# Two of four weight sums added in the transfer, and one block's gating issued after the down round beside it

## The chip, the cores and the metric

The kernel runs on one core of a Trainium2 chip. The metric is the time of one execution on the device in microseconds (us), lower is better. The work is in float32 throughout, and every product is made of three matrix multiplications on split operands, so the result stays near float32 accuracy.

## The reference, cut to what matters

Two layers over 512 tokens of width 1024. Each has a token mixer (layer 0 a spatial gating unit, layer 1 a gated linear recurrence), and then the channel mixer that the change is about:

```python
def conv_ffn(h, w_up, conv_w, conv_b, w_down):      # h: 512 x 1024, w_up: 1024 x 6144, w_down: 3072 x 1024
    up = causal_dwconv(h @ w_up, conv_w, conv_b)    # width 3, per channel
    gate, val = jnp.split(up, 2, axis=-1)
    return (jax.nn.gelu(gate) * val) @ w_down

for i in range(2):
    x = x + mixer(rms_norm(x, norm_mix[i]))
    x = x + conv_ffn(rms_norm(x, norm_ffn[i]), ...)
return rms_norm(x, norm_final)
```

## The kernel before, in words

Features lie on the 128 partitions, the 512 tokens along the free axis. Every float32 operand is split into a high part (a cast to fp32r, `nc.scalar.copy`, on ACT) and a low part (what the cast left out, `tensor_tensor` subtract, on DVE), and a product is high*high + high*low + low*high on PE.

**Up blocks.** `conv_ffn` makes the 3072 hidden channels in 12 blocks, q = 0 to 11. `up(q)` runs 96 matmuls of 512 columns into 4 PSUM banks (gate and value, two groups of 128 channels each). DVE multiplies each bank by the norm factor `rbc` into a tile `up`; ACT and DVE make the width-3 convolution into a tile `cv` (one ACT operation, two DVE `scalar_tensor_tensor`); ACT applies gelu to the gate, and DVE multiplies gate and value into `yr`. `input_sums` then adds and subtracts quarters of `yr` and splits seven of them into the tile `y` (one ACT cast, one long DVE subtract).

**Down rounds.** `down(qs, ...)` multiplies six blocks by `f_w_down` in Winograd's form of Strassen's scheme: `seven` makes 7 products instead of 8, each into its own PSUM bank, of sums of the four quarters of the weights and sums of the four quarters of the input. There are three such rounds: layer 0 after block 6 (blocks 0 to 5) and after block 11 (blocks 6 to 11), and layer 1 after block 6 (blocks 0 to 5). Blocks 6 to 11 of layer 1 go through an ordinary product, `project_out`. Each round runs twice (m = 0, 1) over half of the output columns; a round has 12 chunks, one for each m and block. The names say which: `d0010` is layer 0, the round that begins with block 0, m = 1, block 0, and `d06010` is layer 0, the round that begins with block 6, m = 0, block 10. A chunk is 42 matmuls of 256 columns: 18 read its part a (plain quarters), then 24 its part b (sums of quarters).

**Weights of a chunk.** `weight_sums` loads the four quarters into a tile `raw` (here `d0010r`) by two transfers on the queue of SP, makes four sums on DVE (`d0010s`: one operation over 512 columns, two over 256), and splits part a (three quarters, 768 columns) and part b (four sums, 1024 columns) into `d0010ahi`, `d0010alo`, `d0010bhi`, `d0010blo`. `raw`, high and low tiles each come from a ring of three buffers, which the weights of the up blocks (`fu060r` and so on) use as well. Parts a and b take turns in the ring, so part b of a chunk gets its buffer when PE has read part a of the chunk before it, and part a of a chunk when PE has read part b of the chunk two before it.

**After a round.** Banks are added into the residual `xall` in 11 operations of DVE with two scratch tiles `e` and `u` and two ACT copies.

**Order.** The program is written in one order; a scheduler sets each engine's queue at build time by priorities, and `tc.high_priority` moves weight splitting and the first reads of the banks ahead. On the chip each engine runs its queue strictly in order, and an instruction that waits holds up all behind it.

## Time and profile before

| | |
|---|---|
| median of 3 runs | 1345.16 us (1344.72 to 1346.21) |
| profiled execution, its own time | 1344.57 us |
| its span, first to last instruction | 1342.8 us |
| PE busy | 1319.3 us, 98% of the span |
| DVE busy | 955.9 us, 71% |
| ACT busy | 595.2 us, 44% |
| POOL busy | 12.0 us, 1% |
| mean granted clock of PE | 0.997 of full speed |
| moved by transfers | 129.30 MB, mean 96 GB/s |

PE is busy almost all the time, and the rest of the span is short waits. A time on the chip is the span and some 1.8 us around it. A busy share says little about a stretch: DVE is at 71% over the span, and far above that in some stretches of some 35 us, which the rows below show.

### The profile page before, as it was taken

What the parts mean: (1) busy time and instruction counts of PE and PEld (TensorE: products, weight loads), DVE (VectorE), ACT (ScalarE), POOL (GpSimd) and SP (SyncE); (2) the same over time, 40 slices, a digit from 0 to 9 for tenths busy, and PEclk for the clock granted to TensorE, in tenths of its full rate; (3) what the DMA queues carried; (4) which work ended last, traced back from release to release, by engine and by line L of the source; (5) the groups of instructions that cost most, each with busy time, mean ns of one, the idle gap of its engine ahead of it and who ended that gap; (6) DMA issues with size and microseconds to landing.
All of it is one profiled execution on the core that took longest, in us unless ns stands there. A gap on an engine that the chain in (4) does not pass through costs nothing.

```text
span 1342.8 us, 16731 instructions
## 1 busy us (share of the span) xinstructions
PE 1319.3 (98%) x6510; PEld 1103.8 (82%) x6510; DVE 955.9 (71%) x1336; ACT 595.2 (44%) x773; POOL 12.0 (1%) x20
## 2 busy tenths in 40 slices
PE   9999999999999989999899999999999999999997
PEld 7888888888888988888887888888888899888886
DVE  7227775447878886878987799954687888676735
ACT  6455332334444433444453678633344443343432
POOL 1010000000000000000000000000000000000000
PEclk9999999999999999999999999999999999999999
DMA  6333222222222223222232333223222222422221
GB/s 231 93 94 108 80 79 94 95 94 94 94 95 87 84 82 126 94 92 71 90 118 87 94 94 94 94 97 102 85 94 94 94 79 95 126 94 94 92 82 63
DMA packets 106127, 129.30 MB, mean 96 GB/s; under 512 B 6464, under 2 KB 80192, under 8 KB 106048
## 3 DMA queue, kind: packets, MB, share of 16 engines
q1 hardware_dynamic: 105904, 128.23, 29.8%
q8 instruction: 51, 0.84, 0.3%
q14 instruction: 28, 0.23, 0.1%
q10 hardware_dynamic: 144, 0.00, 0.0%
HBM read 126.11 MB, written 2.10 MB: 95 GB/s over the span
## 4 chain that ended last, share of the span: by engine, by line
PE 90%; DVE 7%; issue 2%; ACT 1%; DVEq 0%; POOLq 0%; POOL 0%; ACTq 0%
PE f L111 13%; PE f L112 13%; PE f L113 13%; PE u L111 2%; PE v L374 2%; PE v L375 2%; PE u L113 2%; PE u L112 2%; PE v L376 2%; PE aop L111 2%; PE aop L113 2%; PE aop L112 2%; PE d001m L515 2%; PE d101m L515 2%; PE bx L113 2%
## 5 line engine op out<-in xcount | busy, mean ns | idle before, releaser
L458 DVE SCALAR_TENSOR_TENSOR cv<-up,vt,cv 128x511 f32<-128x511 f32 (+1 forms) x192 | 141.4, 746 | 20.8 <-ACT cv L456 19.7
L456 ACT ACTIVATE cv<-up,vt 128x512 f32<-128x512 f32 x96 | 77.7, 811 | 84.2 <-DVE up L542 84.2
L542 DVE TENSOR_TENSOR up<-f,rbc 128x512 f32<-128x512 f32 x96 | 65.2, 684 | 0.0
L495 DVE TENSOR_TENSOR y<-yr,y 128x1792 fp32r<-128x1792 f32 x18 | 36.5, 2025 | 13.8 <-ACT y L494 13.8
L546 ACT ACTIVATE cv<-cv 128x512 f32<-128x512 f32 x48 | 30.2, 629 | 33.6 <-DVE cv L458 33.0
L494 ACT CAST y<-yr 128x1792 fp32r<-128x1792 f32 x18 | 30.4, 1690 | 14.1 <-DVE yr L492 8.5
L434 DVE SCALAR_TENSOR_TENSOR sv<-sv,vt,bs 128x256 f32<-128x256 f32 x32 | 15.0, 478 | 19.1 <-PE sv L431 19.1
L211 ACT ACTIVATE xh<-xall,vt 128x512 fp32r<-128x512 f32 x24 | 17.0, 717 | 21.9 <-DVE xall L263 15.9
L220 ACT ACTIVATE sq<-xall 128x512 f32<-128x512 f32 (+1 forms) x37 | 21.4, 586 | 9.8 <-DVE xall L275 9.8
L458 DVE SCALAR_TENSOR_TENSOR xb<-xr,vt,xb 128x511 f32<-128x511 f32 (+2 forms) x36 | 25.5, 744 | 0.1
L548 DVE TENSOR_TENSOR yr<-cv 128x512 f32<-128x512 f32 x36 | 24.8, 688 | 0.8
L221 DVE TENSOR_TENSOR acc<-acc,sq 128x512 f32<-128x512 f32 (+1 forms) x37 | 23.8, 643 | 2.0 <-ACT sq L220 1.9
L212 DVE SCALAR_TENSOR_TENSOR xl<-xall,vt,xh 128x512 fp32r<-128x512 f32 x24 | 17.9, 747 | 3.4 <-ACT xh L211 3.2
L552 ACT CAST y<-cv 128x512 fp32r<-128x512 f32 x12 | 7.4, 620 | 27.5 <-DVE cv L550 23.6
L226 POOL TENSOR_TENSOR rc<-ms,mhalf 128x4 f32<-128x4 f32 (+1 forms) x6 | 5.4, 904 | 1237.3 <-DVE ms L225 1237.3
L430 PE MATMUL sv<-ws,vh 128*128 128x256 f32 x64 | 15.4, 324 | 0.0
L436 DVE SCALAR_TENSOR_TENSOR sv<-sv,vt 128x256 f32<-128x256 f32 x32 | 15.0, 479 | 0.4
L431 PE MATMUL sv<-ws,vl 128*128 128x128 f32 x64 | 14.2, 222 | 0.0
L681 DVE TENSOR_TENSOR_SCAN hs<-riyh,sq 128x512 f32<-128x512 f32 x12 | 14.0, 1208 | 0.0
L490 DVE TENSOR_TENSOR yr<-yr 128x512 f32<-128x512 f32 x18 | 12.5, 692 | 0.6
L86 ACT ACT_TABLE_LOAD x10 | 12.8, 1283 | 0.1
L431 PEld LDWEIGHTS sv<-ws,vl 128*128 128x128 f32 x64 | 12.2, 191 | 0.5
(2559 smaller groups left out, 4475.1 us busy)
## 6 DMA issues: line engine op xcount, KB each, us to landing
xall<-xT SPq DMA_DIRECT2D x8, 256.0 KB, 5.2
outT<-o SPq DMA_DIRECT2D x8, 256.0 KB, 2.2
av00raw<-a_w_in SPq DMA_DIRECT2D x2, 256.0 KB, 3.9
av01raw<-a_w_in SPq DMA_DIRECT2D x2, 256.0 KB, 5.0
av02raw<-a_w_in SPq DMA_DIRECT2D x2, 256.0 KB, 5.6
av03raw<-a_w_in SPq DMA_DIRECT2D x2, 256.0 KB, 5.3
bs<-a_b_s SPq DMA_DIRECT2D x1, 512.0 KB, 6.0
av10r<-a_w_in SPq DMA_DIRECT2D x1, 512.0 KB, 6.6
```

The lines of the kernel that those rows point to most:

```text
L111: nc.tensor.matmul(ps, wh, xh, start=first, stop=False)
L112: nc.tensor.matmul(ps, wh, xl, start=False, stop=False)
L113: nc.tensor.matmul(ps, wl, xh, start=False, stop=last)
L374: nc.tensor.matmul(pss[c], xh[kk][:, ts], hi[:, k, :], start=kk == 0, stop=False)
L375: nc.tensor.matmul(pss[c], xh[kk][:, ts], lo[:, k, :], start=False, stop=False)
L456: nc.scalar.activation(dst, src, AF.Identity, scale=col(wname, woff + last * wstep), bias=col(cname, coff))
L458: nc.vector.scalar_tensor_tensor(dst[:, i:], src[:, :S - i], col(wname, woff + (last - i) * wstep), dst[:, i:], op0=ALU.mult, op1=ALU.add)
L494: nc.scalar.copy(hi, raw[:, 0:7])
L495: nc.vector.tensor_tensor(lo, raw[:, 0:7], hi.bitcast(F32), op=ALU.subtract)
L515: nc.tensor.matmul(banks[b][:, j], wt[:, w, js], xt, start=first and j == 0 and m == 0, stop=last and j == 1 and m == 2, skip_group_check= ...
L542: nc.vector.tensor_tensor(upt, pss[2 * half + j], rbc, op=ALU.mult)
L546: nc.scalar.activation(ts[0], ts[0], AF.Gelu_apprx_tanh)
```

## The change

`weight_sums` gets a tile of five slots in place of four. Write the quarters as (k, n). Two transfers on SP's queue each read one quarter and write it into two slots: (1,0) into slots 1 and 4, (0,1) into slots 0 and 3. A third loads (1,1) into slot 2. Then a transfer issued by POOL (`nc.gpsimd.dma_start` with `accum_op=add`) reads (0,0) and adds it to slots 3 and 4 as it writes them. Slots 0 to 2 are part a, slots 3 and 4 are the first two sums of part b; DVE makes only the other two, over 256 columns each, and part b is split in two pieces of 512 columns. `up` is cut in two: it now ends when the four banks are multiplied by `rbc`, and `gated` does the convolution, gelu and product. For block 6, `up(6)` is written ahead of `down` and `gated(6)` behind it. The scratch tiles `e` and `u` share the one buffer of `yr`; the pool of working tiles has 8 buffers in `conv_ffn` (5 before) and 6 in the first mixer (7 before).

```diff
@@ -147,7 +147,7 @@
     def load_x(k):
         nc.sync.dma_start(xs[k], xT[k * P:(k + 1) * P, :])
 
-    mixer = enter(("yp", 24), ("wk", 7), ("bs", 1))
+    mixer = enter(("yp", 24), ("wk", 6), ("bs", 1))
     bs = phase["bs"].tile([P, AG, P], F32, name="bs")
 
 
@@ -468,22 +468,29 @@
 
 
     def weight_sums(src, name):
-        raw = wp.tile([P, 4, 256], F32, tag="raw", name=f"{name}r")
-        for k in range(2):
-            nc.sync.dma_start(raw[:, 2 * k:2 * k + 2], src[:, k])
-        sums = phase["sm"].tile([P, 4, 256], F32, tag="sm", name=f"{name}s")
-        parts = []
+        raw = wp.tile([P, 5, 256], F32, tag="raw", name=f"{name}r")
+        for k, n, to in ((1, 0, raw[:, 1:5:3]), (0, 1, raw[:, 0:4:3])):
+            nc.sync.dma_start(to, src[:, k, n:n + 1].broadcast_to([P, 2, 256]))
+        nc.sync.dma_start(raw[:, 2], src[:, 1, 1])
+        nc.gpsimd.dma_start(raw[:, 3:5], src[:, 0, 0:1].broadcast_to([P, 2, 256]), accum_op=ALU.add)
+        sums = phase["sm"].tile([P, 2, 256], F32, tag="sm", name=f"{name}s")
+
+        def part(n, t):
+            return tuple(wp.tile([P, n, 256], F32R, tag=g, name=f"{name}{t}{g}", padded_shape=[P, 4, 256]) for g in ("hi", "lo"))
+
+        def fill(hi, lo, src):
+            nc.scalar.copy(hi, src)
+            nc.vector.tensor_tensor(lo, src, hi.bitcast(F32), op=ALU.subtract)
+
         with tc.high_priority(HIGH):
-            nc.vector.tensor_tensor(sums[:, 0:2], raw[:, 1:3], raw[:, 0:1].broadcast_to([P, 2, 256]), op=ALU.add)
-            nc.vector.tensor_tensor(sums[:, 2], raw[:, 1], sums[:, 1], op=ALU.add)
-            nc.vector.tensor_tensor(sums[:, 3], raw[:, 3], sums[:, 2], op=ALU.add)
-            for t, src in (("a", raw[:, 1:4]), ("b", sums)):
-                n = src.shape[1]
-                hi, lo = (wp.tile([P, n, 256], F32R, tag=g, name=f"{name}{t}{g}", padded_shape=[P, 4, 256]) for g in ("hi", "lo"))
-                nc.scalar.copy(hi, src)
-                nc.vector.tensor_tensor(lo, src, hi.bitcast(F32), op=ALU.subtract)
-                parts.append((hi, lo))
-        return parts
+            ah, al = part(3, "a")
+            fill(ah, al, raw[:, 0:3])
+            nc.vector.tensor_tensor(sums[:, 0], raw[:, 0], raw[:, 4], op=ALU.add)
+            nc.vector.tensor_tensor(sums[:, 1], raw[:, 2], sums[:, 0], op=ALU.add)
+            bh, bl = part(4, "b")
+            fill(bh[:, 0:2], bl[:, 0:2], raw[:, 3:5])
+            fill(bh[:, 2:4], bl[:, 2:4], sums)
+        return (ah, al), (bh, bl)
 
 
     def input_sums(raw, dst):
@@ -517,7 +524,7 @@
         return banks
 
     def conv_ffn(l, gain_name, gain_off, chunks):
-        stack = enter(("y", 6), ("yr", 1), ("sm", 1), ("ev", 1), ("wk", 5))
+        stack = enter(("y", 6), ("yr", 1), ("sm", 1), ("wk", 8))
         wu = f_w_up[l].rearrange("(k p) (two n) -> p k two n", p=P, two=2)
         wd = f_w_down[l].rearrange("(k p) (two n) -> p k two n", p=P, two=2)
         ys, plain = {}, []
@@ -531,6 +538,16 @@
                 ], f"fu{l}{q}{kc}")
                 return hi.rearrange("p k h n -> p k (h n)"), lo.rearrange("p k h n -> p k (h n)")
             pss = block(KD, ld, xparts, f"f{q}", norm_hooks if q == 0 else {}, chunks)
+            ups = []
+            for j in range(2):
+                for half in range(2):
+                    upt = work("up")
+                    nc.vector.tensor_tensor(upt, pss[2 * half + j], rbc, op=ALU.mult)
+                    ups.append(upt)
+            return ups
+
+
+        def gated(q, ups):
             y = phase["y"].tile([P, 7, S], F32R, tag="y", name=f"y{q}")
             if q < summed:
                 raw = phase["yr"].tile([P, 8, HS], F32, tag="yr", name=f"yr{q}")
@@ -538,10 +555,8 @@
                 ts = []
                 for half in range(2):
                     f = half * NF + 2 * q + j
-                    upt = work("up")
-                    nc.vector.tensor_tensor(upt, pss[2 * half + j], rbc, op=ALU.mult)
                     t = work("cv")
-                    conv(t, upt, 3, "f_conv_w", "f_conv_b", l * 6 * NF + f, 2 * NF, l * 2 * NF + f)
+                    conv(t, ups[2 * j + half], 3, "f_conv_w", "f_conv_b", l * 6 * NF + f, 2 * NF, l * 2 * NF + f)
                     ts.append(t)
                 nc.scalar.activation(ts[0], ts[0], AF.Gelu_apprx_tanh)
                 if q < summed:
@@ -562,8 +577,8 @@
                               lambda q: wd[:, 2 * q:2 * q + 2, :, m * 256:(m + 1) * 256], f"d{l}{qs[0]}{m}")
                 x2, x1 = xall[:, 2 * m:2 * m + 2, :], xall[:, 4 + 2 * m:6 + 2 * m, :]
                 t0, t1 = slice(0, HS), slice(HS, S)
-                e = phase["ev"].tile([P, 2, S], F32, tag="e", name=f"e{l}{qs[0]}{m}")
-                u = phase["ev"].tile([P, 2, S], F32, tag="u", name=f"u{l}{qs[0]}{m}")
+                eu = phase["yr"].tile([P, 4, S], F32, tag="yr", name=f"e{l}{qs[0]}{m}")
+                e, u = eu[:, 0:2], eu[:, 2:4]
                 with tc.high_priority(HIGH):
                     nc.scalar.copy(e[:, :, t0], banks[1])
                     nc.vector.tensor_tensor(x1[:, :, t0], banks[2], x1[:, :, t0], op=ALU.add)
@@ -586,11 +601,13 @@
                 square(k)
 
         half = NF // 4
-        for q in range(half + 1):
-            up(q)
+        for q in range(half):
+            gated(q, up(q))
+        ahead = up(half)
         down(list(range(half)), None)
+        gated(half, ahead)
         for q in range(half + 1, NF // 2):
-            up(q)
+            gated(q, up(q))
         if gain_name:
             down(list(range(half, NF // 2)), next_norm)
         else:
```

PE's queue holds the same matmuls in the same order. On the other engines the rows move. (Line numbers are those of each version; `xall`, `e`, `u` are the residual and its scratch.)

The first place is DVE's queue at the middle of a round (layer 0, blocks 0 to 5), where m = 0 ends and m = 1 begins. Before:

```order
L484 TENSOR_TENSOR d0010alo<-d0010r,d0010ahi 128x768
L569 TENSOR_TENSOR xall<-d000m_3439,xall 128x2x256
L570 TENSOR_TENSOR xall<-xall,d000m_3440 128x2x256
L571 TENSOR_TENSOR u_3788<-d000m_3441,e_3787 128x2x256
L477 TENSOR_TENSOR d0010s<-d0010r 128x512
L572 TENSOR_TENSOR u_3788<-u_3788,d000m_3442 128x2x256
L478 TENSOR_TENSOR d0010s<-d0010r,d0010s 128x256
L574 TENSOR_TENSOR xall<-d000m_3444,xall 128x2x256
L479 TENSOR_TENSOR d0010s<-d0010r,d0010s 128x256
L575 TENSOR_TENSOR xall<-xall,e_3787 128x1024
L578 TENSOR_TENSOR xall<-xall,u_3788 128x2x256
L484 TENSOR_TENSOR d0010blo<-d0010s,d0010bhi 128x1024
```

After:

```order
L483 TENSOR_TENSOR d0010alo<-d0010r,d0010ahi 128x768
L584 TENSOR_TENSOR xall<-d000m_3409,xall 128x2x256
L585 TENSOR_TENSOR xall<-xall,d000m_3410 128x2x256
L586 TENSOR_TENSOR e_3775<-d000m_3411,e_3775 128x2x256
L483 TENSOR_TENSOR d0010blo<-d0010r,d0010bhi 128x512
L587 TENSOR_TENSOR e_3775<-e_3775,d000m_3412 128x2x256
L483 TENSOR_TENSOR d0010blo<-d0010s,d0010bhi 128x512
L589 TENSOR_TENSOR xall<-d000m_3414,xall 128x2x256
L483 TENSOR_TENSOR d0011alo<-d0011r,d0011ahi 128x768
```

Between the low part of `d0010`'s a and that of its b there stood ten operations (three weight sums, seven over the residual); now there are three, one more stands between b's two pieces, and the weight sums stand ahead of part a.

The second place is ACT's queue in m = 1 of the same round, at the cast into `y` of block 6. Before:

```order
L483 CAST d0011ahi<-d0011r 128x768
L494 CAST y_3403<-yr_3404 128x7x256
L483 CAST d0011bhi<-d0011s 128x1024
L483 CAST d0012ahi<-d0012r 128x768
L483 CAST d0012bhi<-d0012s 128x1024
```

After, at the end of the round and in the up block behind it (`fu070` to `fu073` are the weights of block 7):

```order
L482 CAST d0015bhi<-d0015s 128x512
L99 CAST fu070h<-fu070r 128x1024
L583 COPY e_4155<-d001m_3788 128x2x256
L99 CAST fu071h<-fu071r 128x1024
L588 COPY e_4155<-d001m_3793 128x2x256
L99 CAST fu072h<-fu072r 128x1024
L99 CAST fu073h<-fu073r 128x1024
L501 CAST y_4168<-yr_4169 128x7x256
```

The cast of `y` for block 6 stood between the a and b of chunk `d0011`; it now stands behind the whole round.

The third place is DVE's queue in the round of blocks 6 to 11 of layer 0, at chunk `d06010`. Before:

```order
L484 TENSOR_TENSOR d06010alo<-d06010r,d06010ahi 128x768
L477 TENSOR_TENSOR d06010s<-d06010r 128x512
L491 TENSOR_TENSOR yr_4945<-yr_4945 128x256
L478 TENSOR_TENSOR d06010s<-d06010r,d06010s 128x256
L492 TENSOR_TENSOR yr_4945<-yr_4945 128x256
L479 TENSOR_TENSOR d06010s<-d06010r,d06010s 128x256
L495 TENSOR_TENSOR y_4944<-yr_4945,y_4944 128x7x256
L484 TENSOR_TENSOR d06010blo<-d06010s,d06010bhi 128x1024
```

After:

```order
L483 TENSOR_TENSOR d06010alo<-d06010r,d06010ahi 128x768
L499 TENSOR_TENSOR yr_4984<-yr_4984 128x256
L483 TENSOR_TENSOR d06010blo<-d06010r,d06010bhi 128x512
L483 TENSOR_TENSOR d06010blo<-d06010s,d06010bhi 128x512
L488 TENSOR_TENSOR d06011s<-d06011r 128x256
L489 TENSOR_TENSOR d06011s<-d06011r,d06011s 128x256
L502 TENSOR_TENSOR y_4983<-yr_4984,y_4983 128x7x256
```

The long subtract into `y` (`128x7x256`) stood ahead of `d06010`'s part b, and now stands behind it and behind the next chunk's sums. In this round no gating is moved by the code, since block 11 is gated ahead of it as before.

The rows show one more thing: in the first round of each layer the eight `scalar_tensor_tensor` of block 6's convolution still stand between the weight rows of the round's first four chunks. Behind the round stand, in layer 0, its two products, `input_sums` and the split into `y`; in layer 1 the products stand inside the round too, and only its two subtracts into `y` stand later than before, behind chunk `d1012`.

## Rows read from the trace of the kernel before

**Rows 1.** The page: busy time of each engine, share of span, instructions.
```profile
PE 1319.3 (98%) x6510; PEld 1103.8 (82%) x6510; DVE 955.9 (71%) x1336; ACT 595.2 (44%) x773; POOL 12.0 (1%) x20
```

**Rows 2.** Waits of PE: who waited, for whom, us in total, times, longest.
```profile
PE d001m L515 <- DVE d0011blo L484: 2.6, 1, 2.6
PE d001m L515 <- DVE d0010blo L484: 2.5, 1, 2.5
PE d061m L515 <- DVE d0616alo L484: 2.0, 1, 2.0
PE d060m L515 <- DVE d06010blo L484: 1.9, 1, 1.9
PE d101m L515 <- DVE d1011blo L484: 1.6, 1, 1.6
...
PE d101m L515 <- DVE d1010blo L484: 1.1, 1, 1.1
...
PE d061m L515 <- DVE d0618blo L484: 0.9, 1, 0.9
PE d061m L515 <- DVE d0619blo L484: 0.5, 1, 0.5
PE d061m L515 <- DVE d0617blo L484: 0.4, 1, 0.4
```

**Rows 3.** The chain that ended last, in time: start, us, work.
```profile
482.35 4.34 PE d001m L515 x24
...
491.65 23.30 PE d001m L515 x192
```

**Rows 4.** Stretches: busy us (count) of each engine, clock, share and rate of transfers.
```profile
424.80:447.30 22.50, 22.50 (x98) 18.09 (x97) 19.39 (x29) 9.39 (x12) 0.00 (x0) 1.00 0.24 72
447.30:482.40 35.10, 32.60 (x272) 32.42 (x270) 32.26 (x49) 15.88 (x20) 0.00 (x0) 1.00 0.30 89
482.40:491.70 9.30, 6.74 (x43) 6.54 (x43) 7.01 (x10) 3.37 (x3) 0.00 (x0) 0.82 0.21 64
627.20:664.00 36.80, 32.96 (x271) 32.44 (x269) 33.67 (x50) 17.48 (x21) 0.00 (x0) 1.00 0.25 77
```

**Rows 5.** DVE in time, at the middle of layer 0's first round.
```profile
474.11 0.95 DVE L484 TENSOR_TENSOR d0010alo<-d0010r,d0010ahi 128x768 fp32r<-128x768 f32 x1
474.98 0.68 DVE L569 TENSOR_TENSOR xall<-d000m,xall 128x512 f32<-128x512 f32 x1
475.58 0.68 DVE L570 TENSOR_TENSOR xall<-xall,d000m 128x512 f32<-128x512 f32 x1
...
480.98 1.22 DVE L484 TENSOR_TENSOR d0010blo<-d0010s,d0010bhi 128x1024 fp32r<-128x1024 f32 x1
...
488.43 2.03 DVE L495 TENSOR_TENSOR y<-yr,y 128x1792 fp32r<-128x1792 f32 x1 [2.29 <-ACT y L494]
490.37 1.22 DVE L484 TENSOR_TENSOR d0011blo<-d0011s,d0011bhi 128x1024 fp32r<-128x1024 f32 x1
```

**Rows 6.** DVE in time, one quiet chunk of the same round.
```profile
501.99 0.68 DVE L477 TENSOR_TENSOR d0014s<-d0014r 128x512 f32<-128x512 f32 x1
502.71 0.42 DVE L478 TENSOR_TENSOR d0014s<-d0014r,d0014s 128x256 f32<-128x256 f32 x1
...
504.79 1.23 DVE L484 TENSOR_TENSOR d0014blo<-d0014s,d0014bhi 128x1024 fp32r<-128x1024 f32 x1 [1.19 <-ACT d0014bhi L483]
```

**Rows 7.** Groups of instructions: busy us, mean ns, idle before.
```profile
L553 DVE TENSOR_TENSOR y<-cv,y 128x512 fp32r<-128x512 f32 x12 | 8.2, 687 | 3.5 <-ACT y L552 3.4
```

**Rows 8.** Transfers: issues, KB each, us from issue to landing.
```profile
av10r<-a_w_in SPq DMA_DIRECT2D x1, 512.0 KB, 6.6
...
d0004r<-f_w_down SPq DMA_DIRECT2D x2, 256.0 KB, 3.2
```

**Rows 9.** SP's queue in time: two transfers of one chunk.
```profile
494.05 1.20 SPq L473 DMA_DIRECT2D d0015r<-f_w_down  x2
```

**Rows 10.** DVE in time, ahead of the same round: its first weight sum.
```profile
425.45 0.69 DVE L477 TENSOR_TENSOR d0000s<-d0000r 128x512 f32<-128x512 f32 x1 [0.51 <-DMA d0000r<-f_w_down]
```

## Prediction

> **What bounds the kernel now.** I began with the page's busy times: PE is busy for 98% of the span [rows 1], so little can be won beyond PE's own waits. The second view was the list of those waits. Nine of them, all for the low part of a down round's weights and all on DVE, make 2.6 + 2.5 + 2.0 + 1.9 + 1.6 + 1.1 + 0.9 + 0.5 + 0.4 = 13.5 us [rows 2]. No wait of PE lies in an up block or in the mixers. The third view, the chain, gives the pace of a round without waits: 192 matmuls in 23.30 us, 0.121 us each [rows 3]. A chunk of 42 is thus 5.1 us, its part a (18) 2.2 and its part b (24) 2.9. The same view shows 24 matmuls behind the first wait taking 4.34 us where 2.91 were due, and the stretch around them has a granted clock of 0.82 of full speed where its neighbours have 1.00 [rows 3, 4]: PE had stood still for 2.5 us, and then ran part of it at the lower of its two levels, 1.2 GHz for 2.4. That is 1.4 us more. What the change can touch is therefore 13.5 + 1.4 = 14.9 us.
>
> The fourth view, busy time by stretch, says why DVE is late. In the first half of layer 0's first round DVE is busy 32.3 of 35.1 us, in that of the second round 33.7 of 36.8; take the second round's two waits (1.9 + 2.0) from 36.8 and PE's own work is 32.9, less than what DVE had to do [rows 2, 4]. DVE in time shows the two single causes in the first round. Part a of `d0010` starts at 474.11, and ten operations follow before part b starts at 480.98. Then the subtract into `y` waits 2.29 us for ACT's cast, and `d0011`'s part b, queued behind it, starts only at 490.37 [rows 5]. That cast waits because the buffer of `y` for block 6 is that of block 0, which PE reads until the first chunk of m = 1 is done.
>
> **The sums.** A quiet chunk costs DVE 0.95 for part a, 0.68 + 0.42 + 0.42 for the sums and 1.23 for part b, 3.70 us [rows 5, 6]. After, part a stays, two sums of 0.42 stay, and part b is two subtracts over 512 columns at 0.69 [rows 7]: 3.17. That saves 0.53 a chunk, 19 us over 36 chunks; it counts only where DVE is late. ACT gets one more cast a chunk; even at 0.69 each, seven in the first stretch bring it from 15.9 to 20.7 of 35.1 us [rows 4, 7], so it costs nothing.
>
> **The transfers.** SP issues three a chunk in place of two, at 0.60 each 1.8 of every 5.1 us [rows 9]. Bytes written grow from 512 to 896 KB a chunk; the transfer share of 0.30 becomes 0.53, or 0.68 if the adding transfer counts twice for reading what it adds to [rows 4]. Neither is full, so neither costs.
>
> **The adding transfer** is the unknown: the trace has no transfer issued by POOL. It waits for the two double loads. Behind it on POOL stands only the next one, and after a round the small power of the next norm; the first sum waits for it at the head of DVE's queue, with part a of its chunk behind. Call its time from the loads' landing to its own A. Bounds from the nearest rows: not under 3.2 us, a plain 256 KB load, and 6.6 us for the slowest load, of twice the bytes [rows 8]. I take 4, near the load of its own size, with something for reading the old value. From a `raw` buffer's release to usable sums is then 0.6 (second issue) + 3.2 + A = 7.8 us, between 7.0 and 10.4 [rows 8, 9]. By one page only, the Trainium skill, DMA: Bandwidth & Descriptors, section Anatomy of one DMA, a transfer of the software path takes 2.0 us and its bytes at 436 GB/s; that would make A an estimated 2.6, and the sum would be the same.
>
> When is it due? Count from PE's start on the chunk before chunk n. The buffer is released when b's first piece of n is split: 2.2 until PE has left the previous part a, then a cast and a subtract of some 0.69, 3.6 us. The sums of chunk n + 3 stand in the queue behind b of n + 2, which cannot end before 10.2 + 2.2 + 3 x 0.69 = 14.5. The gap is 10.9 us, more than all of 7.0 to 10.4: DVE does not wait in the steady part. At the head of each round it does. There the first sum ran at 425.45, as soon as its load had landed [rows 10]; now it must wait A = 4 us more, at worst 6.6. DVE has 22.5 - 19.4 = 3.1 us of idle time in that up block [rows 4], and the four multiplications by `rbc` that now come first fill some of the wait. I take nothing; without this cover it would be up to 3 us at each of the three heads.
>
> **The first half-way point, worked out.** Operations over 512 columns start 0.60 apart [rows 5]. From 474.98: three over the residual until 476.8, b's first piece 477.4, one more 478.0, b's second piece 478.6. PE came there at 482.35 - 2.50 = 479.85 [rows 2, 3]. So the 2.5 us go, and the 1.4 us of slow clock with them; layer 1's 1.1 us stand at the same point.
>
> **The convolution put behind.** Its eight operations stay inside the round, as the rows of the change show. What leaves it in layer 0 is two products, `input_sums` and the long subtract, some 5 us of DVE, and above all the cast that waited for PE. Then `d0011`'s part b has in front of it, from 478.6: one operation over the residual, part a, two sums, one over 1024 columns, a piece of b and one more, some 5 us, done at 483.7. PE gets there at 479.85 + 2.9 + 2.2 = 484.95. The 2.6 us go, with 1.3 us to spare; 1.6 us in layer 1, where the two subtracts into `y` moved behind the next chunk. The work lands in the up block behind the round, where DVE has its 3.1 us of room, and so has each of the four after it; without that cover it would cost its 5 us once.
>
> **The second round.** Nothing is moved there by hand. Seven chunks x 0.53 = 3.7 us less bring DVE to 30.0 us against 32.9 of PE [rows 4], and the long subtract no longer stands ahead of `d06010`'s part b. So 1.9 + 2.0 go. The last three (0.4, 0.9, 0.5) add up to 1.8 over three chunks that save 1.6; the residual's first reads also come in another order. I count them as gone and keep up to 2 us for the range.
>
> **Pools.** `e` and `u` in `yr`'s buffer wait for block 5's or 11's `y`, which PE needs before it makes what `e` reads; six working tiles in the first mixer meet a PE that never waits there [rows 2]. Nothing.
>
> **Sum.** 1344.57 - 14.9 = 1329.7 on the profiled execution, which was 0.6 under the median of 1345.16: 1330.3.
>
> **Rivals.** (1) *Slower: the adding transfer is longer than the ring.* A buffer's cycle is 0.6 + 3.2 + A, then two sums, part a and b's first piece (0.42 + 0.42 + 0.95 + 0.69 = 2.5), and has three chunks, 15.3 us. From A = 9.0 on, each further us costs a third of a us in 36 chunks, 12 us. The gain is gone at A = 10.2; A = 11 gives 1330.3 + 24 = 1354. Against it: that is 1.5 times the slowest row. For it: no row shows such a transfer. Chance 0.11.
> (2) *POOL and DVE hold each other up.* If each adding transfer held DVE for as long as one operation over 512 columns, 0.69, the 0.53 saved would be lost. The second round would keep its 5.7 us of waits, and only 14.9 - 5.7 = 9.2 would be won: 1336. DVE runs only operations on two tensors in these rounds [rows 5, 6]. A page speaks to this by a rule: the Trainium skill, SBUF — State Buffer, section Who interferes with whom, says that operations in the two-port modes (copy, cast, and one tensor with a scalar) lock GpSimd out, so that it cannot write descriptors, and that a `tensor_tensor` contends only with GpSimd's reads. By that rule the rounds are free of it; no run here shows either yet. Chance 0.13.
> (3) *Waits only shorten or move*, since a queue in strict order passes one late row on: half the sum, 7 us, 1338. For it: the 1.3 us to spare above. Chance 0.08.
> (4) *No change*: A of some 10, where (1) eats what is won, or DVE late at each round's head: 1345. Chance 0.05.
>
> The forecast has 0.63. A range of 1327.5 to 1342 holds it, (2) and (3), 0.84, with some of the forecast's tails outside; the bounds of A alone move nothing. Within 0.2%, 2.7 us, is about what a measurement cannot tell from no change. Faster 0.84, same 0.05, slower 0.11.
>
> **What would show it.** Right: no wait of PE on `d0010`, `d0011` or `d06010` parts b, a clock of 1.00 through the round, DVE's first sums not waiting on a transfer except at a round's head, and POOL's transfers landing in 3 to 7 us. Wrong: waits of DVE on the adding transfer in every chunk (1), longer operations on DVE (2), or PE waiting on other parts of the same rounds (3).

## The result and the profile after

The changed kernel takes 1327.52 us (median of 4 runs, 1327.02 to 1328.25) where the kernel before takes 1345.68 beside it (1344.72 to 1347.06): a ratio of 0.9865, 95% interval 0.9848 to 0.9882. That is 18.2 us less, and 16.3 on the profiled executions (1328.25 against 1344.57): the profiled one of the kernel before lies 1.1 under its median, that of the changed kernel 0.7 over its own, and there the first up block started 0.7 us later. The forecast was 1330.3, in a range of 1327.5 to 1342.

The page's busy times of the changed kernel, as in [rows 1]: PE has 1316.4 of a span of 1326.5 us, DVE 20.7 less work than before, POOL the issues of 36 transfers more.

```profile
PE 1316.4 (99%) x6510; PEld 1103.5 (83%) x6510; DVE 935.2 (71%) x1336; ACT 600.6 (45%) x809; POOL 54.3 (4%) x56
```

The list of PE's waits, beside [rows 2]. None of the nine waits of the down rounds is left; these three lie at the start and the end of the program and stood there before.

```profile
PE rb L298 <- DVE dg L291: 1.5, 1, 1.5
PE warm L158 <- DVE warm L155: 1.3, 1, 1.3
PE st L287 <- ACT sq L277: 1.0, 1, 1.0
```

The chain through layer 0's first round (start, us, work). It is PE from end to end; 18 matmuls of a part a take 2.17 us, and 234 run on in 28.31, 0.121 each, as in the undisturbed piece of [rows 3].

```profile
448.18 7.19 PE d000m L522 x60
455.38 23.30 PE d000m L522 x192
478.68 2.17 PE d001m L522 x18
480.94 28.31 PE d001m L522 x234
```

Busy time by stretch (columns as in [rows 4]): the four halves of layer 0's two rounds. The clock is 1.00 where [rows 4] has 0.82 behind the first wait; the transfer share is 0.67 to 0.70, the double count that the prediction gave as 0.68.

```profile
447.30:478.70 31.40, 31.39 (x258) 31.04 (x257) 25.94 (x45) 17.02 (x26) 6.66 (x6) 1.00 0.68 168
478.70:509.30 30.60, 30.49 (x253) 30.30 (x253) 24.42 (x40) 13.17 (x20) 4.08 (x4) 1.00 0.67 167
621.70:652.00 30.30, 30.30 (x255) 30.30 (x254) 29.31 (x49) 18.36 (x27) 7.00 (x6) 1.00 0.68 165
652.00:682.20 30.20, 30.20 (x253) 30.19 (x252) 26.95 (x44) 17.83 (x28) 3.73 (x4) 1.00 0.70 166
```

DVE in time, the place of [rows 5]: it stands idle for 2.25 us ahead of the first sum of `d0010`, for the adding transfer, and is done with the second piece of part b at 480.80; PE began that part at 480.94.

```profile
475.44 0.43 DVE L488 TENSOR_TENSOR d0010s<-d0010r 128x256 f32<-128x256 f32 x1 [2.25 <-issue]
475.90 0.42 DVE L489 TENSOR_TENSOR d0010s<-d0010r,d0010s 128x256 f32<-128x256 f32 x1
476.25 0.95 DVE L483 TENSOR_TENSOR d0010alo<-d0010r,d0010ahi 128x768 fp32r<-128x768 f32 x1
...
478.91 0.68 DVE L483 TENSOR_TENSOR d0010blo<-d0010r,d0010bhi 128x512 fp32r<-128x512 f32 x1
...
480.11 0.69 DVE L483 TENSOR_TENSOR d0010blo<-d0010s,d0010bhi 128x512 fp32r<-128x512 f32 x1
```

Transfers between 440 and 510 us: the queues (packets, MB, share of the engines), and issue to landing as in [rows 8]. The adding transfers take 3.9 to 6.5 us; the plain loads of the round's weights, 3.1 to 4.2 before, now take 3.1 to 5.8.

```profile
q0 software_dynamic: 2720, 2.62, 25.1%
...
d0013r<-f_w_down SPq DMA_DIRECT2D x2, 256.0 KB, 5.4
...
d0004r<-f_w_down POOLq DMA_DIRECT2D x1, 256.0 KB, 6.5
d0005r<-f_w_down POOLq DMA_DIRECT2D x1, 256.0 KB, 3.9
...
d0015r<-f_w_down SPq DMA_DIRECT2D x1, 128.0 KB, 5.8
```

The table below holds for every kernel of this study what PE needed for each half of a round, from its first matmul on the half's first chunk to its first on what follows (us, from the traces). A half without waits takes 30.1 to 30.3. The stages between are the same to 0.1 us in all kernels (up blocks 158.9, 112.5, 158.9 and 112.4, the mixer between the layers 235.0), but for 0.6 more in that mixer where the table says so, and 0.4 with two raw buffers. What lies ahead of the first up block and behind the last differs by up to 1.0 us from trace to trace.

| kernel | L0 round 1 | | L0 round 2 | | L1 round | | median, us |
|---|---|---|---|---|---|---|---|
| before | 30.2 | 37.2 | 34.6 | 32.8 | 30.3 | 33.5 | 1345.68 |
| changed | 30.5 | 30.5 | 30.3 | 30.1 | 30.3 | 30.1 | 1327.52 |
| sums alone | 30.2 | 30.1 | 30.2 | 30.1 | 30.3 | 30.1 | 1327.14 |
| move alone | 30.3 | 32.3 | 34.5 | 32.8 | 30.5 | 33.9 | 1340.52 |
| no adding transfer | 30.2 | 30.1 | 30.2 | 30.1 | 30.2 | 30.2 | 1326.98 |
| cut, all sums on DVE | 30.3 | 30.1 | 30.2 | 31.2 | 30.2 | 30.1 | 1330.09 (mixer +0.6) |
| cut alone | 30.2 | 30.1 | 30.3 | 31.5 | 30.2 | 30.2 | 1329.83 (mixer +0.6) |
| cast alone cut | 30.3 | 36.4 | 32.3 | 37.3 | 30.3 | 30.9 | 1345.14 |
| sums, one piece | 30.2 | 35.6 | 31.2 | 32.4 | 30.3 | 31.9 | 1337.70 |
| change, one piece | 30.3 | 31.6 | 32.0 | 32.4 | 30.4 | 32.3 | 1335.82 |
| part a written first | 30.2 | 38.9 | 32.3 | 35.9 | 30.3 | 33.5 | 1347.11 |
| adding twice | 43.9 | 46.3 | 41.8 | 44.8 | 42.9 | 46.3 | 1413.36 |
| two raw buffers | 38.9 | 38.6 | 43.0 | 38.7 | 36.7 | 39.4 | 1385.20 |
| plain POOL transfer | 30.3 | 30.1 | 30.3 | 30.1 | 30.2 | 30.2 | 1327.98 |

Over the six halves the kernel before loses 17.7 us against 30.15 each, and the changed one 0.9: the 16.8 between them is the gain. [Rows 2] and the slow clock had 14.9 of it.

### The profile page after: what moved, and what is told of

Its sections match the earlier page's. It is cut to its first block, busy times and chain, and to the rows that moved or that the text cites. A ratio compares the mean times of both kernels' runs of the same rounds, so it can differ in the third digit from the quotient of the medians.

```text
span 1326.5 us, 17029 instructions
## 1 busy us (share of the span) xinstructions
PE 1316.4 (99%) x6510; PEld 1103.5 (83%) x6510; DVE 935.2 (71%) x1336; ACT 600.6 (45%) x809; POOL 54.3 (4%) x56
## 3 DMA queue, kind: packets, MB, share of 16 engines
q1 hardware_dynamic: 111088, 132.95, 31.5%
## 4 chain that ended last, share of the span: by engine, by line
PE 99%; issue 1%; DVE 0%; DVEq 0%; POOLq 0%; POOL 0%
PE f L111 14%; PE f L112 14%; PE f L113 14%; PE v L374 2%; PE d000m L522 2%; PE d001m L522 2%; PE v L375 2%; PE u L111 2%; PE d101m L522 2%; PE d061m L522 2%; PE d100m L522 2%; PE d060m L522 2%; PE u L113 2%; PE u L112 2%; PE v L376 2%; PE aop L111 2%
## 5 line engine op out<-in xcount | busy, mean ns | idle before, releaser
L458 DVE SCALAR_TENSOR_TENSOR cv<-up,vt,cv 128x511 f32<-128x511 f32 x192 | 135.8, 745 | 0.7
L545 DVE TENSOR_TENSOR up<-f,rbc 128x512 f32<-128x512 f32 x96 | 63.7, 686 | 35.6 <-PE f L113 33.2
L456 ACT ACTIVATE cv<-up,vt 128x512 f32<-128x512 f32 x96 | 70.7, 804 | 0.5 <-DVE up L545 0.5
L561 ACT ACTIVATE cv<-cv 128x512 f32<-128x512 f32 x48 | 30.3, 632 | 34.4 <-DVE cv L458 34.3
L501 ACT CAST y<-yr 128x1792 fp32r<-128x1792 f32 x18 | 30.4, 1691 | 14.3 <-DVE yr L499 14.3
```

The costliest lines, as they stand in the source:

```text
L456: nc.scalar.activation(dst, src, AF.Identity, scale=col(wname, woff + last * wstep), bias=col(cname, coff))
L458: nc.vector.scalar_tensor_tensor(dst[:, i:], src[:, :S - i], col(wname, woff + (last - i) * wstep), dst[:, i:], op0=ALU.mult, op1=ALU.add)
L501: nc.scalar.copy(hi, raw[:, 0:7])
L545: nc.vector.tensor_tensor(upt, pss[2 * half + j], rbc, op=ALU.mult)
L561: nc.scalar.activation(ts[0], ts[0], AF.Gelu_apprx_tanh)
```

## The experiments

**The sums alone.** The kernel before with the new `weight_sums` (and six working tiles in the first mixer); `up`, `down` and the pools of the feed-forward stay.

```diff
-        raw = wp.tile([P, 4, 256], F32, tag="raw", name=f"{name}r")
+        raw = wp.tile([P, 5, 256], F32, tag="raw", name=f"{name}r")
...
+        nc.gpsimd.dma_start(raw[:, 3:5], src[:, 0, 0:1].broadcast_to([P, 2, 256]), accum_op=ALU.add)
...
+            fill(bh[:, 0:2], bl[:, 0:2], raw[:, 3:5])
+            fill(bh[:, 2:4], bl[:, 2:4], sums)
```

> The new sums with the adding transfer, and the convolution left ahead of the down round as before. By the prediction's steps the sums carry the first half-way points and the second round, and the convolution put behind carries the waits on d0011 b (2.6 us) and d1011 b (1.6): 4.2 us of the gain go, about 1332. By the order of rows the long subtract into y has slid by itself from ahead of d0011 b to between the two pieces of d0012 b, some five operations later: then hardly any wait is left, at most 1 us on d0012, and the time is 1328 to 1330. Rival (the moved convolution is the whole gain): 1342 to 1345, with waits on d0010 b and d0011 b as before.

Measured: 1327.14 us, ratio 0.9861 (0.9848 to 0.9875), no wait in any round. The sums alone do all that the change does. DVE in time shows where the long subtract went without being moved by hand: in [rows 5] it stood ahead of `d0011`'s part b, here it stands between the two pieces of `d0012`'s.

```profile
482.49 0.68 DVE L483 TENSOR_TENSOR d0011blo<-d0011s,d0011bhi 128x512 fp32r<-128x512 f32 x1
...
485.84 0.68 DVE L483 TENSOR_TENSOR d0012blo<-d0012r,d0012bhi 128x512 fp32r<-128x512 f32 x1
486.44 2.02 DVE L502 TENSOR_TENSOR y<-yr,y 128x1792 fp32r<-128x1792 f32 x1
488.38 0.68 DVE L483 TENSOR_TENSOR d0012blo<-d0012s,d0012bhi 128x512 fp32r<-128x512 f32 x1
```

**The move alone.** The changed kernel with the `weight_sums` of before (and seven working tiles in the first mixer): the convolution behind the round, the scratch shared.

```diff
-            bh, bl = part(4, "b")
-            fill(bh[:, 0:2], bl[:, 0:2], raw[:, 3:5])
-            fill(bh[:, 2:4], bl[:, 2:4], sums)
...
+            nc.vector.tensor_tensor(sums[:, 0:2], raw[:, 1:3], raw[:, 0:1].broadcast_to([P, 2, 256]), op=ALU.add)
...
+            for t, src in (("a", raw[:, 1:4]), ("b", sums)):
```

> The convolution put behind the round and the shared scratch, with the four sums on DVE as before. Theory (DVE's load decides in the second round, the order in the first): the waits of the second round stay (2.0, 1.9, 0.9, 0.5, 0.4, some 7 us of PE's time), that of layer 1 shrinks, those of the first round go: 1335 to 1338. Rival (lighter sums are all that counts): near 1345, with the wait on d0010 b kept. Rival (the order is all that counts): 1328.

Measured: 1340.52, ratio 0.9961 (0.9948 to 0.9975): 5.2 us by the ratio, less than expected. The first round's second half loses 2.2 us in place of 7.0, the second round keeps its losses to 0.1, as expected; layer 1 loses 0.6 more than before, which was not: its first wait grew from 1.1 to 2.3 us.

```profile
PE d101m L515 <- DVE d1010blo L484: 2.3, 1, 2.3
PE d061m L515 <- DVE d0616alo L484: 2.0, 1, 2.0
...
PE d001m L515 <- DVE d0011blo L484: 1.0, 1, 1.0
```

**No adding transfer.**

```diff
-        nc.gpsimd.dma_start(raw[:, 3:5], src[:, 0, 0:1].broadcast_to([P, 2, 256]), accum_op=ALU.add)
```

> The changed kernel without the adding transfer: the first two parts lack the quarter (0,0), so their values are others; every other instruction is kept. Theory (DVE's waits of 0.8 to 2.3 us on the adding transfer lie in time that DVE has over): the time of the changed kernel, 1327 to 1328.5, and those waits of DVE are gone or put down to PE and ACT. Rival (the transfer, or its bytes, still costs somewhere): 1324 to 1326.

Measured: 1326.98, ratio 0.9860 (0.9846 to 0.9873), which is the changed kernel's. The transfer's latency, its bytes and POOL's issues cost PE nothing that can be measured. DVE's waits ahead of the first sums are gone; ahead of part a it now waits 0.87 to 0.93 us for ACT's cast in five chunks of the first round.

**The adding transfer twice.**

```diff
         nc.gpsimd.dma_start(raw[:, 3:5], src[:, 0, 0:1].broadcast_to([P, 2, 256]), accum_op=ALU.add)
+        nc.gpsimd.dma_start(raw[:, 3:5], src[:, 0, 0:1].broadcast_to([P, 2, 256]), accum_op=ALU.add)
```

> The adding transfer made twice, the second waiting for the first: the first two parts get the quarter (0,0) twice, so their values are others. It doubles A. Theory: A measured 3.9 to 6.5 us, some 5, becomes some 10; from a buffer's release to usable sums 10.8 us becomes 15.8, and with 2.5 of DVE's work the ring's cycle is 18.3 us against three chunks of 15.3; 3 us over in 12 cycles is 36 us: 1364, between 1345 and 1380, PE waiting on DVE in nearly every chunk. By the prediction's own sizes (0.6 + 3.2 + A + 2.5 with A = 10, 1 us over the threshold): 1340. Rival (the transfer is never in the way): 1328.

Measured: 1413.36, ratio 1.0501 (1.0481 to 1.0520): 86 us more than the changed kernel, far over all three expectations. POOL in time (its idle time in brackets) shows a mechanism that none of them had. The second issue waits, in POOL's queue, until the first has landed, 6.2 to 6.3 us in these rows, and the next chunk's first issue stands behind it: one chunk every 8.6 us here, every 7.0 to 9.0 over the rest of the round, where PE wants one every 5.1. So this run is no test of the ring.

```profile
459.32 1.28 POOL L475 DMA_DIRECT2D d0004r<-f_w_down  x1
466.88 1.20 POOL L476 DMA_DIRECT2D d0004r<-f_w_down  x1 [6.27 <-DMA d0004r<-f_w_down]
467.60 1.69 POOL L475 DMA_DIRECT2D d0005r<-f_w_down  x1
475.50 1.20 POOL L476 DMA_DIRECT2D d0005r<-f_w_down  x1 [6.20 <-DMA d0005r<-f_w_down]
```

**Two raw buffers.** The ring itself, shortened: the sums alone, with `bufs=2` at every tile of the tag `raw`.

```diff
-        raw = wp.tile([P, 5, 256], F32, tag="raw", name=f"{name}r")
+        raw = wp.tile([P, 5, 256], F32, tag="raw", bufs=2, name=f"{name}r")
```

> The new sums on the kernel before, with two buffers for raw weights in place of three everywhere. A test of the ring's law in rival 1. With what was measured (10.8 us from a buffer's release to usable sums, 2.5 of DVE's work behind) a cycle is 13.3 us against two chunks of 10.2: 1.55 us a chunk, 56 us over 36 chunks, a little less for the two loads ahead at each round's head: 1365 to 1385, all of it in the down rounds. With the prediction's sizes (7.8 + 2.5 = 10.3): 1329. Rival (the wait for the adding transfer has enough cover elsewhere): 1327 to 1330.

Measured: 1385.20 (two executions, 1382.32 and 1388.07), ratio 1.0291 (1.0265 to 1.0316). Against the sums alone that is 58 us, and 54 in the table's halves, which come from the shorter execution; the law with measured sizes said 56. The up blocks and mixers lost at most 0.4. The granted clock is 0.88 to 0.96 in these halves; what of the loss is the clock's is not told apart. DVE's idle time ahead of a first sum is 4.69 and 5.64 us two chunks apart:

```profile
464.75 0.42 DVE L488 TENSOR_TENSOR d0003s<-d0003r 128x256 f32<-128x256 f32 x1 [4.69 <-issue]
...
479.57 0.43 DVE L488 TENSOR_TENSOR d0005s<-d0005r 128x256 f32<-128x256 f32 x1 [5.64 <-issue]
```

**A plain transfer in its place.** The sums alone, without the adding.

```diff
-        nc.gpsimd.dma_start(raw[:, 3:5], src[:, 0, 0:1].broadcast_to([P, 2, 256]), accum_op=ALU.add)
+        nc.gpsimd.dma_start(raw[:, 3:5], src[:, 0, 0:1].broadcast_to([P, 2, 256]))
```

> The new sums on the kernel before, with the adding transfer a plain one of the same bytes, from the same queue and behind the same waits: the first two parts are then the quarter (0,0) alone, so the values are others. Theory (the adding costs the engines a read of what lies there, and is hidden): the time is that of the sums alone, 1327; a transfer lands in 3 to 4 us in place of 3.9 to 6.5, and its share of the engines per byte falls to that of the plain loads, about half. Rival (the time of POOL's transfers is that of its queue, not of the adding): 4 to 6.5 us as before.

Measured: 1327.98, ratio 0.9866 (0.9848 to 0.9884), the same time. Of the ten transfers of POOL in this stretch nine land in 3.1 to 4.0 us and one in 6.3. The same 2.62 MB take 11.4% of the engines where the adding ones took 25.1%:

```profile
q0 software_dynamic: 800, 2.62, 11.4%
...
d0005r<-f_w_down POOLq DMA_DIRECT2D x1, 256.0 KB, 6.3
```

**The cut, with all sums on DVE.** After the sums alone had done everything, the question was which part of them. This is the kernel before with part b cut into two pieces and part a written first as in the change, but with four plain loads and four sums on DVE (and six working tiles in the first mixer).

```diff
+        raw = wp.tile([P, 4, 256], F32, tag="raw", name=f"{name}r")
+        for k, n, to in ((1, 0, raw[:, 1]), (0, 1, raw[:, 0]), (1, 1, raw[:, 2]), (0, 0, raw[:, 3])):
+            nc.sync.dma_start(to, src[:, k, n])
...
+            nc.vector.tensor_tensor(sums[:, 0:2], raw[:, 0:2], raw[:, 3:4].broadcast_to([P, 2, 256]), op=ALU.add)
...
+            fill(bh[:, 0:2], bl[:, 0:2], sums[:, 0:2])
+            fill(bh[:, 2:4], bl[:, 2:4], sums[:, 2:4])
```

> The kernel before with the second part cut into two pieces as in the change, but all four sums on DVE, from four plain loads of 128 KB: the order and the cut without DVE's relief. Theory (the second round needs the relief of DVE): its waits stay, some 7 us of PE's time, and the first round keeps up to 3 us, since DVE is as late as before there: 1334 to 1338. Rival (the cut and the new order of rows do it): 1327 to 1328.5.

Measured: 1330.09, ratio 0.9880 (0.9866 to 0.9893), between the two expectations. My theory at that point, that the second round needs DVE's relief, falls: most of the gain is there with no relief at all.

**The sums in one piece.** The reverse, on the sums alone: adding transfer and relief kept, part b made in one piece (the last two sums written in place, so that its quarters lie side by side).

```diff
+            nc.vector.tensor_tensor(raw[:, 2], raw[:, 2], raw[:, 1], op=ALU.add)
+            nc.vector.tensor_tensor(raw[:, 3], raw[:, 4], raw[:, 2], op=ALU.add)
             bh, bl = part(4, "b")
-            fill(bh[:, 0:2], bl[:, 0:2], raw[:, 3:5])
-            fill(bh[:, 2:4], bl[:, 2:4], sums)
+            fill(bh, bl, raw[:, 0:4])
```

> The adding transfer and two sums of DVE as in the change, the convolution ahead of the round as before, but the second part split as one piece of 1024 columns: the last two sums are written in place so that its four quarters lie side by side. DVE's relief is about the same (its two pieces start 1.20 us apart in all, one piece 1.14). The order of rows then has the long subtract into y ahead of d0011 b again, as in the kernel before. Theory (that wait is one of order, not of load): d0011 b waits some 2.6 us again, d1011 b less, and the rest is gone: 1330 to 1333. Rival (the relief is all that counts): 1327 to 1328.5.

Measured: 1337.70, ratio 0.9939 (0.9926 to 0.9953): less than half the gain. Expected were 1330 to 1333. The wait on `d0011` came back as expected, with a slow clock (0.95 over that half), and so did smaller ones in the second round that I had not expected:

```profile
PE d001m L520 <- DVE d0011blo L482: 2.8, 1, 2.8
...
PE d061m L520 <- DVE d0617blo L482: 0.9, 1, 0.9
PE d060m L520 <- DVE d06010blo L482: 0.7, 1, 0.7
```

**The cut alone.** The smallest edit: the kernel before, its loads, sums and order of code kept.

```diff
-                nc.scalar.copy(hi, src)
-                nc.vector.tensor_tensor(lo, src, hi.bitcast(F32), op=ALU.subtract)
+                for s in (slice(0, 2), slice(2, 4)) if t == "b" else (slice(0, 3),):
+                    nc.scalar.copy(hi[:, s], src[:, s])
+                    nc.vector.tensor_tensor(lo[:, s], src[:, s], hi[:, s].bitcast(F32), op=ALU.subtract)
```

> The kernel before with one edit: the cast and the subtract of the second part are made in two pieces of 512 columns, as in the change; its loads, its four sums on DVE and its convolution stay. DVE gets slightly more to do (two starts of 0.60 in place of one of 1.14), so by the prediction's step of DVE's load nothing is won: 1345. Theory formed after the run with four sums on DVE (1330.1): PE waited for the chain from the last sum over ACT's cast of 1024 columns to DVE's subtract, and for the rows that stood ahead of it; in pieces ACT casts one while DVE subtracts the other: 1328 to 1332, with DVE busy for over 29 us of a half round of 30.2 and PE not waiting.

Measured: 1329.83, ratio 0.9881 (0.9867 to 0.9894): 15.6 us of gain from this edit. Its page has DVE at 956.7 us, no less than [rows 1], and the busy time by stretch has DVE at 29.33 of 30.30 us in the second round's first half, with no wait of PE there; in the second half, at 30.89 of 31.50, DVE is the limit, and 1.4 us are lost.

```profile
PE 1316.6 (99%) x6510; PEld 1101.9 (83%) x6510; DVE 956.7 (72%) x1372; ACT 601.8 (45%) x809; POOL 12.1 (1%) x20
```

```profile
620.40:650.70 30.30, 30.30 (x254) 30.26 (x253) 29.33 (x48) 16.27 (x25) 0.00 (x0) 1.00 0.28 88
650.70:682.20 31.50, 30.68 (x253) 30.27 (x252) 30.89 (x53) 18.57 (x29) 0.00 (x0) 1.00 0.37 114
```

DVE in time at the place of [rows 5]. Part b of `d0010` starts 2.7 us behind its part a, where it was 6.9 before: the weight sums of `d0010` now stand ahead of its part a, three operations over the residual ahead of its first piece, and the others come behind. The first piece needs only the first sums; at `d0011` and `d0012` it runs ahead of the last sum. The long subtract starts at 486.81, behind all of `d0011`.

```profile
473.68 0.96 DVE L485 TENSOR_TENSOR d0010alo<-d0010r,d0010ahi 128x768 fp32r<-128x768 f32 x1 [0.15 <-ACT d0010ahi L484]
...
476.35 0.69 DVE L485 TENSOR_TENSOR d0010blo<-d0010s,d0010bhi 128x512 fp32r<-128x512 f32 x1
476.94 0.69 DVE L573 TENSOR_TENSOR u<-u,d000m 128x512 f32<-128x512 f32 x1
477.54 0.69 DVE L485 TENSOR_TENSOR d0010blo<-d0010s,d0010bhi 128x512 fp32r<-128x512 f32 x1
...
482.74 0.69 DVE L485 TENSOR_TENSOR d0011blo<-d0011s,d0011bhi 128x512 fp32r<-128x512 f32 x1
...
486.81 2.02 DVE L496 TENSOR_TENSOR y<-yr,y 128x1792 fp32r<-128x1792 f32 x1
...
495.50 0.69 DVE L477 TENSOR_TENSOR d0014s<-d0014r 128x512 f32<-128x512 f32 x1
...
497.02 1.46 DVE L485 TENSOR_TENSOR d0014blo<-d0014s,d0014bhi 128x512 fp32r<-128x512 f32 x2
```

The last two rows are the quiet chunk of [rows 6]. From its first sum to the end of part b DVE takes 2.98 us (495.50 to 498.48), where it took 4.03 before (501.99 to 506.02): the 1.19 us for which it stood idle for ACT's cast are gone.

**The cast alone cut.** Does ACT's shorter cast do it, or DVE's rows?

```diff
-                nc.scalar.copy(hi, src)
+                for s in (slice(0, 2), slice(2, 4)) if t == "b" else (slice(0, 3),):
+                    nc.scalar.copy(hi[:, s], src[:, s])
                 nc.vector.tensor_tensor(lo, src, hi.bitcast(F32), op=ALU.subtract)
```

> The kernel before with ACT's cast of the second part in two pieces of 512 columns, DVE's subtract in one of 1024. It tells apart two things that the cut in both brings: ACT can cast the first piece while DVE still makes the last sums (the chain from the last sum to the split part gets some 0.4 us shorter, 1.05 us of cast against 0.62), and the rows on DVE change, so that the long subtract no longer stands ahead of d0011 b and d06010 b. Here the first is there, and the long subtract stands where it stood before. If the shorter chain decides: 1328 to 1333. If the place of the rows on DVE decides: 0.4 us off each of nine waits at most, 1341 to 1345, with the waits on d0011 b and d06010 b left at some 2 us.

Measured: 1345.14, ratio 0.9991 (0.9982 to 1.0000): nothing that can be told from no change. DVE's rows stand in nearly their old order, with the long subtract, 1.42 us of waiting for its cast ahead of it, in front of `d06010`'s part b; DVE still stands idle 0.69 us for ACT in a quiet chunk. The waits lie partly at other chunks (`d0011` has 3.6 us, `d0616`'s part b 2.9), and the halves lose 16.6 us where they lost 17.7.

```profile
647.41 2.02 DVE L496 TENSOR_TENSOR y<-yr,y 128x1792 fp32r<-128x1792 f32 x1 [1.42 <-ACT y L495]
649.35 1.22 DVE L485 TENSOR_TENSOR d06010blo<-d06010s,d06010bhi 128x1024 fp32r<-128x1024 f32 x1
```

**The change in one piece.** The changed kernel with the one-piece sums.

> The changed kernel, but the second part split as one piece of 1024 columns (the last two sums written in place, as in the run with one piece and the convolution left in its place, 1337.7). Theory: the wait of 2.8 us on d0011 b there, and the slow clock behind it, came from the long subtract into y ahead of it; with the convolution behind the round that goes, and the smaller waits of 0.3 to 1.0 stay, above all the second round's: 1332 to 1334. Rival (the long subtract has nothing to do with it, one piece is simply late): 1337. Rival (with the adding transfer and the move both, the cut does nothing): 1327 to 1328.5.

Measured: 1335.82, ratio 0.9928 (0.9915 to 0.9940). Moving the convolution does take the 4 us out of the first round that the long subtract cost there, with the slow clock behind that wait (35.6 to 31.6 in the table; the wait on `d0011` is 0.4, the clock 1.00), but the second round and layer 1 lose 1.3 us more, and in all it is 1.9 (2.6 in the halves). Expected were 1332 to 1334.

**Part a written first.** A control: the cast and subtract of part a ahead of the sums, nothing else.

```diff
             for t, src in (("a", raw[:, 1:4]), ("b", sums)):
+                if t == "b":
+                    nc.vector.tensor_tensor(sums[:, 0:2], raw[:, 1:3], raw[:, 0:1].broadcast_to([P, 2, 256]), op=ALU.add)
...
```

> A control: the kernel before with the first part's cast and subtract written ahead of the four sums, as in the change; the second part stays one piece, and its sums stay on DVE. Theory (the cut decides): 1343 to 1347, with the long subtract ahead of d0011 b and d06010 b as before. Rival (what is written first decides): under 1338.

Measured: 1347.11, ratio 1.0008 (0.9999 to 1.0018), no change; the wait on part a of `d0616` moved to its part b, and the long subtract stays ahead of the parts that it stood ahead of.

## Why the prediction was right in its time and in part wrong in its cause

**The sum, 14.9 us: mis-sized by what a wait costs.** All nine waits went, the clock stayed at 1.00, and the halves gave back 16.8. The list counts a wait from the modelled end of the last matmul, which is later than the moment at which the next was due. In PE's time before the change, at the wait of 0.86 on `d0618`:

```profile
674.65 0.40 PE L515 MATMUL d061m<-y,d0618ahi 128*128 128x256 f32 x2
675.91 0.39 PE L515 MATMUL d061m<-y,d0618blo 128*128 128x256 f32 x1 [0.86 <-DVE d0618blo L484]
676.14 0.41 PE L515 MATMUL d061m<-y,d0618bhi 128*128 128x256 f32 x2
```

Two matmuls from 674.65 take 0.24, so the next was due at 674.89 and came 1.02 late, not 0.86; the one behind it came 0.23 later in place of 0.12. This listed wait thus cost some 0.27 more. If each of the nine did, an estimate from this one place, they make 2.4, and 14.9 + 2.4 = 17.3 stands against the 17.7 of the table; in the run with the move alone, ten waits of 10.2 us in all give 12.9 against 13.4.

**"The sums save 0.53 a chunk, 19 us over 36 chunks": the size holds, its use does not.** DVE's busy time fell by 20.7. But the step let this relief carry the second round, with 33.7 us of DVE's work brought to 30.0 against 32.9 of PE. The cut alone, with DVE no less busy, gives 15.6 us. The relief without the cut (the sums in one piece) gives 8.2 by its ratio and still loses 3.3 of the second round's 7.1. Both act on the same waits, so the two do not add up.

The step that failed is the measure of DVE's lateness. The 3.70 us that "a quiet chunk costs DVE" and the 33.7 against 32.9 of the second round add up busy times alone. In [rows 6] DVE also stands idle for 1.19 us ahead of part b, for ACT's cast of 1024 columns, and the prediction put this term at nothing without a reason. The cut takes 1.05 us off the same rows (4.03 to 2.98), the relief was to take 0.53 off. Over the whole second round DVE has 61.0 us of work before and 60.2 with the cut alone, close to the 60.3 that PE needs for two halves without waits; but it stands idle for ACT's casts for 6.1 us before and for 1.3 with the cut. So DVE was late less from its work than from idle time and from the order of its rows. In [rows 5] the long subtract waits 2.29 us for ACT and takes 2.03 in front of a part that PE needs, while PE needs its own output only in the next round. In the second round the same row stood ahead of `d06010`'s part b, and the next chunk's part b waited again:

```profile
648.34 2.03 DVE L495 TENSOR_TENSOR y<-yr,y 128x1792 fp32r<-128x1792 f32 x1 [1.43 <-ACT y L494]
650.28 1.22 DVE L484 TENSOR_TENSOR d06010blo<-d06010s,d06010bhi 128x1024 fp32r<-128x1024 f32 x1
...
655.08 1.23 DVE L484 TENSOR_TENSOR d06011blo<-d06011s,d06011bhi 128x1024 fp32r<-128x1024 f32 x1 [1.19 <-ACT d06011bhi L483]
```

PE's wait of 1.9 us ends with the second of these rows, and its wait of 2.0 us comes one chunk behind the third, on `d0616`. With the cut already there, the relief adds what the cut alone leaves: 1.4 us in the second round's last half and 0.6 in the mixer behind, 2.0; the two ratios, 0.9881 and 0.9861, say 2.7, and the rest is within what the program's ends differ from trace to trace.

**The cut itself** was in the prediction only as a price, 1.23 us against two operations of 0.69. Its effect on the order stood in the rows of the change, and I read it there for `d0010`, `d0011` and `d06010` without asking which of the edits made it. What the cut does in time is shown: the residual's operations and the long subtract slide behind the pieces, at `d0011` and `d0012` the first piece runs ahead of the last sum, and DVE hardly stands idle for the cast any more. That ACT's shorter cast is not enough by itself is shown by the run with the cast alone cut. That the order of DVE's rows decides is argued: in the run with the cut alone the order, the finer work and the idle time change together. Not tried: one piece with its row put by hand where the pieces stand, so it stays open how much of the 15.6 comes from each.

**That the time came out right is in part luck.** The forecast counted every wait as gone, and every wait went, but through an edit that it had priced only as a small loss. What it had counted on, relief and move, is the run with the change in one piece: 1335.82, 9.7 us of gain by the ratio, where 14.9 were forecast.

**"The convolution put behind": not needed, nor harmful.** Without it the time is the same (0.9861 against 0.9865). The step's chain, cast held by PE and subtract held by the cast, is real: with one piece the wait on `d0011` is 2.8 us with the convolution in place and 0.4 with it moved. But the new sums, cut in two, had removed the wait already. Alone, the move gives 5.2 us, against the 4.2 that the step credits to it.

**The adding transfer: time bounded rightly, its place not.** A was taken as 4 us between 3.2 and 6.6 and is 3.9 to 6.5. The plain loads slowed at a share of 0.67, to 5.8 us at most, where the run without the adding transfer has them at 2.9 to 3.3 and one at 4.5; from the issue for `d0005` (459.47) to its first sum (470.24) it is 10.8 us, over the bound of 10.4. So "DVE does not wait in the steady part" is wrong: it stands idle for 0.8 to 2.3 us ahead of the first sum in six of the first round's twelve chunks, besides the head. Without the transfer these waits are gone and the kernel is no faster: DVE has the time over. They leave little to spare: the matmuls on part b of `d0001` and `d0010` start 0.17 and 0.27 us late, too little for the list, and those behind them 0.1 each: most of the 0.7 us by which the changed kernel's first round is slower than that of the sums alone. By the Trainium skill, DMA: Bandwidth & Descriptors, section Anatomy of one DMA, A was an estimated 2.6; the plain transfer from POOL's queue took 3.1 to 4.0 here, the adding one up to 6.5, and the measurement decides.

**The rivals.** (1) The ring: the run with two buffers bears its law out (54 to 58 us against 56), but three buffers give it 15.3 us against 10.8 + 2.5 = 13.3. (2) POOL and DVE do not hold each other up: the multiplication by `rbc` takes 686 ns after, 684 before, with POOL issuing 36 transfers more, and the rounds' own rows are as long as before (0.42 to 0.43, 0.68 to 0.69, 0.95). That agrees with what the rule cited in the prediction from the Trainium skill, SBUF — State Buffer, section Who interferes with whom, says of `tensor_tensor`. (3) Waits that move: not in the changed kernel, but in the runs with one piece, with the move alone and with the cast alone cut.

**Pools, SP and ACT** cost nothing, as the prediction had it: no wait of PE in the rounds is put down to them.

## What to carry to other kernels

A busy share of 90% and more says that an engine has little over, not that its load is what others wait for: look first at which rows stand ahead of the awaited one, whether those are needed yet, and how long the engine stands idle for another between them. Cutting a long two-engine step into pieces can be worth more than taking work away (15.6 against 8.2 us here): one engine works on a piece while the other makes the next, and other rows can go between. When an edit bundles three ideas, run each alone; here the one that looked like bookkeeping gives 15.6 of the 18.2 us by itself.

## What the runs showed of the hardware

An adding transfer from POOL's queue takes 2.2 times the engine share of a plain one of the same bytes (25.1% against 11.4% for 2.62 MB, in 2720 packets against 800) and lands in 3.9 to 6.5 us against 3.1 to 4.0, with one of 6.3. In the profile POOL is held for 1.2 to 1.4 us by each adding issue (1.7 where it stands right behind another) and for 0.7 to 0.9 by a plain one. An issue that waits for the landing of the one before it holds all issues behind it: 7.0 to 9.0 us a chunk for two in a row. Plain loads beside the adding transfers landed in 3.1 to 5.8 us, and without them in 2.9 to 3.3, with one of 4.5.
